# A split-precision decoder trunk: the first weight sum by an adding DMA, one more Strassen pair per unit, Strassen's products in the branch and first output unit

## The chip, the cores and the metric

One core of one Trainium2 chip. The time is the device time of one execution in microseconds. Engines are named as the profile does: PE (TensorE matmuls), PEld (its weight loads), DVE (VectorE), ACT (ScalarE), POOL (GpSimd), SP (SyncE, which issues most DMAs).

## The reference

One layer, 256 rows of width 4096, all in float32:

```python
u = rmsnorm(h, norm_w)
proj = u @ w_in                        # 4096 x 24576
a_q, a_f, a_i, a_g, b_q, b_k, b_v, b_g, gate_a, gate_b = jnp.split(proj, ...)
o_a = rmsnorm(hgrn2_mix(a_q, a_f, a_i, lb)) * silu(a_g)            # 16 heads of 128
o_b = rmsnorm(diff_attention(b_q, b_k, b_v, lam, slopes)) * 0.8 * silu(b_g)   # 8 heads of 256
y = sigmoid(gate_a) * (o_a @ w_branch_a) + sigmoid(gate_b) * (o_b @ w_branch_b)
out = rmsnorm(h + y @ w_out, final_w)
```

Nearly all the work is the four weight products: 256 rows against 512 MB of weights, each used once.

## The kernel before

**Pieces.** All weights are laid out on the host as 512 pieces, "pairs": two blocks of 128 rows of k beside two blocks of 512 columns, that is 128 partitions x 2048 floats (1 MB), the four blocks of 512 in the order B12, B11, B21, B22. Pairs are grouped in units of 1024 output columns. In order: 16 mixer units of 16 pairs (8 groups of two; the first 4 groups feed the recurrence, the next 4 the attention), 8 gate units of 16, 8 half branch units of 8 (4 branch units, each first a then b), 4 output units of 16. `plan` lists them and `run` walks it: per pair it asks for loads up to `LOAD_AHEAD` pairs ahead, splits chunks up to `stream.ahead` ahead, issues the matmuls, then `post(n)` and one or two items of the queue `todo` (`later`, `step`). Items that use PE run only at pairs 14, 15, 0, 1 and 2.

**Split precision.** A float32 weight w is used as hi + lo, each rounded for the fast matmul format: ACT copies hi (L165), DVE forms lo = w - hi (L166). The left operands (u, o, y) are held as hi and lo too, and each block product is three matmuls: hi by hi, hi by lo, lo by hi (`mm`, L289), 512 columns each, into one of 8 PSUM banks.

**Plain and Strassen pairs.** The output of a unit is 2 row blocks x 2 column blocks, banks 0 to 3. A plain pair has two chunks (one per k block) of 1024 columns; each chunk goes to four banks, 24 matmuls in all. A pair of kind "S" is multiplied by Strassen's scheme in Winograd's form: seven block products, 21 matmuls, into banks 0, 1, 2 and P1, p5, P6, P7, with four chunks (1024, 1024, 512 and 1024 columns) in the order of `ORDER`. Its weight sums are made by DVE in `sums`: w0 + w1 (L146), T = w0 - w3 into a tile of its own (L147), and T taken from w1 and w2 at once (L151). Its left sums are formed once per k pair in `s_form` (four DVE operations of 128x128, a copy by ACT, a difference by DVE) and kept in the pools `sp` and `sp2`. The product banks P1 to P7 are evicted after the unit's last S pair into four tiles of the pool `gp` (L313 to L324) and added to banks 0 to 3 at the unit's end. Kinds before: 6 S pairs (`SPLIT`) in mixer units 3 to 15 and gate units 0 and 1; 9 (`SPLIT_G`) in gate units 2 to 6; none in gate unit 7 and the branch units; none in the first output unit and 7 (`Y_SPLIT`) in the three others. 156 of 512.

**Queues and buffers.** Raw pieces have 3 buffers (`wraw`), filled by SP's queue, one DMA per pair except at the start; a buffer is free when the pair's last chunk is split. Split chunks have 5 pairs of tiles in the mixers and 7 afterwards. POOL's queue stores the gates, o, y and h to DRAM, loads y, and masks scores. The order of instructions on each engine is made by a scheduler at build time; splits and evictions get priority (`tc.high_priority`).

**Ends of units.** The last pair of a unit is held and its four blocks are finished one by one, so that banks finish some 1.4 us apart. In the branch units the two halves use different sets of four banks (`bank2`, `bank`), as does the first output unit.

Of the kernel before, what the change touches and what calls it, by code (L numbers as in the profile page):

```python
# [17 lines left out]
P = 128  # L18
D = 4096
S = 256  # L20
# [17 lines left out]
SPLIT_AHEAD = 3  # L38
# [5 lines left out]
def trunk_kernel(ctx, tc, xT, x, nw, w_mix, w_gate, w_branch, w_out, lbt, hnw, lamv, slw, fw, out):  # L44
# [8 lines left out]
    wt = ctx.enter_context(tc.tile_pool(name="wt", bufs=1))  # L53
    sp = ctx.enter_context(tc.tile_pool(name="sp", bufs=6))
# [6 lines left out]

    def bank2(b):
        return bank(("P1", "p5", "P6", "P7")[b])
# [32 lines left out]
    class Stream:  # L96
# [3 lines left out]

        def __init__(self):
# [19 lines left out]
        def load_to(self, n):  # L121
            while self.loaded < min(n, len(self.src)):
# [19 lines left out]
        def sums(self, i, c):  # L142
            w = self.raw[i]
            if c == 0:
                t = self.raw[i, "T"] = wt.tile([P, 512], F32, name="wt", tag="wt")
                dve.tensor_tensor(w[:, 0:512], w[:, 0:512], w[:, 512:1024], op=ALU.add)  # L146
                dve.tensor_tensor(t, w[:, 0:512], w[:, 1536:2048], op=ALU.subtract)  # L147
            if c == 2:
                t = self.raw[i, "T"]
                b = w[:, 512:1536].rearrange("p (a c) -> p a c", a=2)  # L150
                dve.tensor_tensor(b, b, t.unsqueeze(1).to_broadcast([P, 2, 512]), op=ALU.subtract)  # L151

        def split_to(self, n):
            while self.done < min(n, len(self.chunks)):
# [12 lines left out]
                if c == (3 if self.kind[i] == "S" else 1):  # L167
                    del self.raw[i]
                    self.raw.pop((i, "T"), None)
# [96 lines left out]
    ORDER = (("p5", "P1"), (0, 1), ("P6",), ("P7", 2))  # L266
# [4 lines left out]
    def wide_unit(srcs, kinds, pf, sf, bank, final, post=None, tail=1, kt0=0, pre=None):  # L271
# [62 lines left out]
        def fn(n, c, hi, lo):  # L334
            if pre and c == 0:
                pre(n)
            if kinds[n] == "S":
                for i, b in enumerate(ORDER[c]):
# [4 lines left out]
                    else:  # L343
                        s = {"p5": 0, "P6": 1, "P7": 2, 1: 3}[b]
                        uh, ul = (sf[n][:, s, a, :] for a in range(2))
# [8 lines left out]
            for blocks in ([[(t, m)] for t in range(2) for m in range(2)] if tail == 1  # L354
# [86 lines left out]
    SPLIT = (4, 6, 8, 10, 12, 13)  # L441
    SPLIT_G = (0, 2, 4, 6, 8, 10, 12, 13, 14)
    us = {}
    s_pools = [sp] * 6
# [19 lines left out]
    def more_sums(n):  # L464
        if n == 0:
            s_pools[:] = [sp2] * 3
# [4 lines left out]
    oh, ol = [], {}  # L471
# [559 lines left out]
```

## Time and profile before

| | |
|---|---|
| median of 3 runs | 2794.47 us (2794.36 to 2796.64) |
| the profiled execution | 2795.3 us, its span 2793.6 us |
| granted PE clock | 0.999 |
| busy share PE / PEld / DVE / ACT / POOL | 99% / 82% / 79% / 57% / 3% |
| HBM read, written | 571.5 MB, 24.1 MB |
| DMA share of SP's queue, of POOL's queue | 56.3%, 2.8% |

The span runs from the first to the last instruction; the execution's time has 1.7 us around it. In a row of instructions the figures are the count, busy time in us, mean ns of one, idle time of the engine just before them, and what ended that idle time. A window row gives, for a stretch, its length, then busy us and count per engine, the granted clock, the DMA engines' mean busy share, and GB/s. Matmuls overlap in PE's pipeline: a row of 0.39 us is one matmul's way through, and the time from one to the next is shorter.

### The profile page before, as it was taken

To read this page: it belongs to the slowest core of one execution; us is meant where nothing else is said; L and a number is where in the kernel's file an instruction comes from. 1 tells how busy PE (TensorE), PEld (TensorE's weight loads), DVE (VectorE), ACT (ScalarE), POOL (GpSimd) and SP (SyncE) were. 2 spreads that over 40 slices of the span, in tenths; PEclk is the share of its full clock that TensorE was granted. 3 is DMA by queue.
4 is the path that set the end of the run, shared out by engine and by line. 5 is a ranking of instruction groups with operands and counts; after the bars stand their busy time and mean duration, and the time that the engine had idled before them with its cause. 6 is when DMAs were issued, how large, how long until landed. Compare 5 with 4: busy or idle time off the path is not lost.

```text
span 2793.6 us, 32659 instructions
## 1 busy us (share of the span) xinstructions
PE 2770.9 (99%) x12418; PEld 2285.5 (82%) x12418; DVE 2219.3 (79%) x2502; ACT 1578.5 (57%) x1877; POOL 75.0 (3%) x124
## 2 busy tenths in 40 slices
PE   9999999999999999999999999999999999999998
PEld 7888888888888888888888888778888888888886
DVE  6784888888888888888888999999855555668997
ACT  7664656556556555565556555555553444445554
POOL 0010000000000000000000000000000000010000
PEclk9999999999999999999999999999999999999999
DMA  9555555554555555555456555555676666665665
GB/s 351 190 179 192 181 195 189 211 203 181 196 189 208 198 177 203 194 198 201 181 192 239 224 199 208 226 219 203 253 260 220 230 223 234 240 244 212 249 250 217
DMA packets 96767, 597.76 MB, mean 214 GB/s; under 512 B 11857, under 2 KB 12129, under 8 KB 31201
## 3 DMA queue, kind: packets, MB, share of 16 engines
q1 hardware_dynamic: 88272, 566.29, 56.3%
q0 software_dynamic: 8336, 29.38, 2.8%
q8 instruction: 97, 1.59, 0.2%
q14 instruction: 62, 0.50, 0.1%
HBM read 571.51 MB, written 24.12 MB: 213 GB/s over the span
## 4 chain that ended last, share of the span: by engine, by line
PE 84%; DVE 10%; DMA 3%; issue 1%; ACT 1%; POOL 0%; DVEq 0%; ACTq 0%; POOLq 0%
PE ps_w L289 82%; DVE lo L166 7%; DMA w<-in_w_gate 2%; DVE w L151 1%; ACT hi L165 1%; DMA w<-in_w_out 1%; DVE w L146 1%; PE ps_q L742 1%; DVE wt L147 0%; PE ps_sc L825 0%; PE ps_s L906 0%; DVE ut L372 0%; PE ps_o L840 0%; PE ps_y L541 0%; PE ps_t L701 0%
## 5 line engine op out<-in xcount | busy, mean ns | idle before, releaser
L165 ACT ACTIVATE hi<-w 128x1024 fp32r<-128x1024 f32 (+1 forms) x1184 | 1215.1, 1053 | 1073.9 <-PE ps_w L289 598.4
L166 DVE TENSOR_TENSOR lo<-w,hi 128x1024 fp32r<-128x1024 f32 (+1 forms) x1184 | 1415.4, 1219 | 437.1 <-ACT hi L165 423.8
L289 PE MATMUL ps_w<-hi,u 128*128 128x512 f32 x4794 | 1538.4, 391 | 1.7 <-ACT hi L165 1.6
L289 PEld LDWEIGHTS ps_w<-hi,u 128*128 128x128 f32 x4794 | 900.1, 188 | 190.3 <-ACT hi L165 3.0
L289 PE MATMUL ps_w<-lo,u 128*128 128x512 f32 x2397 | 935.0, 390 | 0.9 <-DVE lo L166 0.9
L289 PEld LDWEIGHTS ps_w<-lo,u 128*128 128x128 f32 x2397 | 450.2, 188 | 98.2 <-DVE lo L166 6.5
L289 PE MATMUL ps_w<-hi,sf 128*128 128x512 f32 x1248 | 437.0, 390 | 0.7 <-ACT hi L165 0.7
L289 PE MATMUL ps_w<-hi,oh 128*128 128x512 f32 x1024 | 317.1, 390 | 0.0
L289 PEld LDWEIGHTS ps_w<-hi,sf 128*128 128x128 f32 x1248 | 234.3, 188 | 50.1 <-ACT hi L165 1.4
L289 PE MATMUL ps_w<-hi,y 128*128 128x512 f32 x814 | 258.1, 389 | 0.0
L289 PE MATMUL ps_w<-lo,sf 128*128 128x512 f32 x624 | 244.3, 392 | 4.9 <-DVE lo L166 4.6
L289 PEld LDWEIGHTS ps_w<-hi,oh 128*128 128x128 f32 x1024 | 192.3, 188 | 39.6
L289 PE MATMUL ps_w<-lo,oh 128*128 128x512 f32 x512 | 199.2, 389 | 0.0
L151 DVE TENSOR_TENSOR w<-w,wt 128x1024 f32<-128x1024 f32 x156 | 190.4, 1220 | 0.3
L289 PEld LDWEIGHTS ps_w<-hi,y 128*128 128x128 f32 x814 | 152.8, 188 | 31.6
L289 PE MATMUL ps_w<-lo,y 128*128 128x512 f32 x407 | 158.4, 389 | 0.0
L289 PEld LDWEIGHTS ps_w<-lo,sf 128*128 128x128 f32 x624 | 117.1, 188 | 34.4 <-DVE lo L166 10.5
L146 DVE TENSOR_TENSOR w<-w 128x512 f32<-128x512 f32 x156 | 107.4, 690 | 46.5 <-DMA w<-in_w_mix 33.3
L165 ACT ACTIVATE hi<-wt 128x512 fp32r<-128x512 f32 x156 | 97.9, 627 | 36.9 <-PE ps_w L289 23.0
L289 PEld LDWEIGHTS ps_w<-lo,oh 128*128 128x128 f32 x512 | 96.2, 188 | 19.8
L147 DVE TENSOR_TENSOR wt<-w 128x512 f32<-128x512 f32 x156 | 107.5, 689 | 2.6
L166 DVE TENSOR_TENSOR lo<-wt,hi 128x512 fp32r<-128x512 f32 x156 | 107.1, 686 | 0.0
(206 smaller groups left out, 1040.6 us busy)
## 6 DMA issues: line engine op xcount, KB each, us to landing
w<-in_w_mix SPq DMA_DIRECT2D x252, 1024.0 KB, 4.8
w<-in_w_gate SPq DMA_DIRECT2D x128, 1024.0 KB, 4.9
w<-in_w_branch SPq DMA_DIRECT2D x64, 1024.0 KB, 4.9
w<-in_w_out SPq DMA_DIRECT2D x64, 1024.0 KB, 4.9
gl<-g_dram SPq DMA_DIRECT2D x32, 256.0 KB, 2.7
g_dram<-ut POOLq DMA_DIRECT2D x28, 256.0 KB, 5.3
o_dram<-s POOLq DMA_DIRECT2D x8, 512.0 KB, 6.0
ol<-o_dram SPq DMA_DIRECT2D x16, 256.0 KB, 5.4
```

The costliest lines, as they stand in the source:

```text
L146: dve.tensor_tensor(w[:, 0:512], w[:, 0:512], w[:, 512:1024], op=ALU.add)
L147: dve.tensor_tensor(t, w[:, 0:512], w[:, 1536:2048], op=ALU.subtract)
L151: dve.tensor_tensor(b, b, t.unsqueeze(1).to_broadcast([P, 2, 512]), op=ALU.subtract)
L165: act.activation(hi[:, k : k + m], t[:, k : k + m], AF.Copy)
L166: dve.tensor_tensor(lo[:, k : k + m], t[:, k : k + m], f32(hi[:, k : k + m]), op=ALU.subtract)
L289: pe.matmul(ps[b], a, w, start=first, stop=left[b] == 0)
L742: pe.transpose(ps[:, j], r[:, j * P : (j + 1) * P], ident)
```

## The change

The first weight sum w0 + w1 is no longer made by DVE: an S pair's load is cut into its first 512 columns and the other 1536, and a third DMA, issued by POOL with addition, reads w1 from DRAM a second time and adds it onto w0 in the buffer. The second sum is written over w3 in place, after the chunk that needs the raw w2 and w3; the chunk order changes so that this raw chunk comes first. `SPLIT` gets 7 pairs, `SPLIT_G` 10 (no longer pair 0, but 1); the branch halves get 2 S pairs each, the first output unit 3. Tiles of the mixers go (the sums of squares are made by ACT's accumulation, scaling is one DVE operation per segment, other tiles are used again), the splits run four chunks ahead there, and blocks finish in the order (0,1), (0,0), (1,1), (1,0), which is also that of the first use in the next unit. Both sets of banks are no longer exchanged.

```diff
-SPLIT_AHEAD = 3
+SPLIT_AHEAD = 4
...
     def load_to(self, n):
...
-                if i > 1:
+                if self.kind[i] == "S":
+                    self.load_part(i, 0, 512)
+                    self.load_part(i, 512, PIECE - 512)
+                    pool.dma_start(t[:, 0:512], self.src[i][:, 512:1024], accum_op=ALU.add)
+                elif i > 1:
...
-        def sums(self, i, c):
+        def sums(self, i):
             w = self.raw[i]
-            if c == 0:
-                t = self.raw[i, "T"] = wt.tile([P, 512], F32, name="wt", tag="wt")
-                dve.tensor_tensor(w[:, 0:512], w[:, 0:512], w[:, 512:1024], op=ALU.add)
-                dve.tensor_tensor(t, w[:, 0:512], w[:, 1536:2048], op=ALU.subtract)
-            if c == 2:
-                t = self.raw[i, "T"]
-                b = w[:, 512:1536].rearrange("p (a c) -> p a c", a=2)
-                dve.tensor_tensor(b, b, t.unsqueeze(1).to_broadcast([P, 2, 512]), op=ALU.subtract)
+            t2 = w[:, 1536:2048]
+            dve.tensor_tensor(t2, w[:, 0:512], t2, op=ALU.subtract)
+            b = w[:, 512:1536].rearrange("p (a c) -> p a c", a=2)
+            dve.tensor_tensor(b, b, t2.unsqueeze(1).to_broadcast([P, 2, 512]), op=ALU.subtract)
...
+                    o = c * HALF
                     if self.kind[i] == "S":
-                        self.sums(i, c)
-                    t = self.raw[i, "T"] if c == 2 else self.raw[i][:, (0, 1024, 0, 512)[c] :]
+                        if c == 2:
+                            self.sums(i)
+                        o = (1024, 0, 1536, 512)[c]
+                    t = self.raw[i][:, o:]
...
-    ORDER = (("p5", "P1"), (0, 1), ("P6",), ("P7", 2))
+    ORDER = ((0, 1), ("p5", "P1"), ("P6",), ("P7", 2))
...
-                plain(n, c, hi, lo, [(0, 0), (0, 1), (1, 0), (1, 1)] if c else [(0, 1), (1, 1), (0, 0), (1, 0)])
+                plain(n, c, hi, lo, [(t, m if c else 1 - m) for t in range(2) for m in range(2)])
...
-            for blocks in ([[(t, m)] for t in range(2) for m in range(2)] if tail == 1
+            for blocks in ([[(t, 1 - m)] for t in range(2) for m in range(2)] if tail == 1
...
-    SPLIT = (4, 6, 8, 10, 12, 13)
-    SPLIT_G = (0, 2, 4, 6, 8, 10, 12, 13, 14)
+    SPLIT = (4, 6, 7, 9, 10, 12, 13)
+    SPLIT_G = (1, 3, 4, 6, 7, 9, 10, 12, 13, 14)
...
+    SPLIT_B = (3, 5)
...
-        p_form(oh[n // 2], 2 * (n % 2), ol.pop(n))
+        f = ol.pop(n)
+        p_form(oh[n // 2], 2 * (n % 2), f)
+        if n % 8 in SPLIT_B:
+            os[n] = s_form(f)
...
+        def gated(t, n, ps, c, dst):
+            if c is not None:
+                dve.tensor_tensor(c, ps, c, op=ALU.add)
+                ps = c
+            dve.tensor_tensor(dst, ps, g[t, n], op=ALU.mult)
...
-        wide_unit([w_branch[0, q, n] for n in range(8)], PLAIN[:8], oh, None, bank2, a_final, post)
-        wide_unit([w_branch[1, q, n] for n in range(8)], PLAIN[:8], oh, None, bank, b_final, post_b, kt0=16)
+        wide_unit([w_branch[0, q, n] for n in range(8)], mix(8, SPLIT_B), oh, os, bank, a_final, post)
+        wide_unit([w_branch[1, q, n] for n in range(8)], mix(8, SPLIT_B), oh, os, bank, b_final, post_b, kt0=16)
...
-        kinds = PLAIN if q == 0 else mix(16, Y_SPLIT)
-        wide_unit([w_out[q, n] for n in range(16)], kinds, y, ys, bank if q else bank2, final, post, 3 if q == 3 else 1)
+        kinds = mix(16, Y_SPLIT if q else Y_SPLIT[4:])
+        wide_unit([w_out[q, n] for n in range(16)], kinds, y, ys, bank, final, post, 3 if q == 3 else 1)
...
             def apply():
-                o3 = fl(o).rearrange("p (n c) -> p n c", c=seg)
-                dve.tensor_tensor(o3, o3, T["ss"].unsqueeze(2).to_broadcast([P, n, seg]), op=ALU.mult)
-                dve.tensor_tensor(fl(o), fl(o), fl(T["silu"]), op=ALU.mult)
+                for i in range(n):
+                    c = slice(i * seg, (i + 1) * seg)
+                    dve.scalar_tensor_tensor(fl(o)[:, c], fl(o)[:, c], ss[:, i : i + 1], fl(T["silu"])[:, c],
+                                             op0=ALU.mult, op1=ALU.mult)
...
-                    act.activation(rows(T["o"])[:, tb], pf, AF.Copy)
-                    act.activation(rows(T["sq"])[:, tb], pf, AF.Square)
+                    o = rows(T["o"])[:, tb]
+                    for h in range(HPG):
+                        i = tb * HPG + h
+                        act.activation(o[:, h * P : (h + 1) * P], ps[:, h], AF.Square, accum_out=T["ss"][:, i : i + 1])
+                    act.activation(o, pf, AF.Copy)
```

In the branch units the four row sums of a and b are now queued as one item (`add_rows`) ahead of the four transposes, which use the spare banks.

More of the change, by code (lines that the diff above doesn't have):

```diff
@@ L517, in branch_unit @@
     def branch_unit(q):
-        rows, g = {}, {}
+        rows, g, merge = {}, {}, []
         def g_load(br):
@@ L614, in final @@
                 last_rows[t, n] = tile_
-                if n == 1:
+                if (t, 1 - n) in last_rows:
                     out_rows(t)
-            if t == 0 and n == 1:
+            del xr[t, n]
+            if t == 0 and not xr:
                 io_x(1)
@@ L748, in final @@
                     T["gv"[n]] = big("gv"[n])
-                if t == 1 and n == 1:
+                if t == 1 and n == 0:
                     for f in then:
```

110 lines of the change are left out of this document (57 added, 53 removed).

## The prediction

> **What bounds the kernel now.** Read first: the share of each engine and the chain that ended last.
>
> ```profile
> span 2793.6 us, 32659 instructions
> PE 2770.9 (99%) x12418; PEld 2285.5 (82%) x12418; DVE 2219.3 (79%) x2502; ACT 1578.5 (57%) x1877; POOL 75.0 (3%) x124
> PE 84%; DVE 10%; DMA 3%; issue 1%; ACT 1%; POOL 0%; DVEq 0%; ACTq 0%; POOLq 0%
> PE ps_w L289 82%; DVE lo L166 7%; DMA w<-in_w_gate 2%; DVE w L151 1%; ACT hi L165 1%; DMA w<-in_w_out 1%; DVE w L146 1%; PE ps_q L742 1%; DVE wt L147 0%; PE ps_sc L825 0%; PE ps_s L906 0%; DVE ut L372 0%; PE ps_o L840 0%; PE ps_y L541 0%; PE ps_t L701 0%
> ```
>
> TensorE's weight matmuls are the chain for 82% of the span; VectorE's split of the weights is 7%. Where that 7% lies is asked of the stages, by windows cut where the count of L289's matmuls says a unit begins (366 for a mixer unit, 357 for gate units 2 to 6, 192 for half a branch unit, 363 for an output unit).
>
> ```profile
> core 0: us, PE busy (x) PEld busy (x) DVE busy (x) ACT busy (x) POOL busy (x), PEclk, DMA share, GB/s
> 1587.63:1668.55 80.92, 80.92 (x359) 67.01 (x357) 75.85 (x85) 47.90 (x56) 1.61 (x3) 1.00 0.60 219
> 1668.55:1751.85 83.30, 82.34 (x358) 66.63 (x357) 78.61 (x85) 48.32 (x56) 2.16 (x4) 1.00 0.57 214
> 1751.85:1835.12 83.27, 82.11 (x359) 66.64 (x357) 77.92 (x85) 50.40 (x58) 2.16 (x4) 1.00 0.56 214
> 1835.12:1920.15 85.03, 82.46 (x358) 66.54 (x357) 80.36 (x88) 47.84 (x55) 2.16 (x4) 1.00 0.57 212
> 1920.15:2003.01 82.86, 82.15 (x358) 66.63 (x357) 77.87 (x84) 51.00 (x57) 2.16 (x4) 1.00 0.58 215
> 2003.01:2090.99 87.98, 87.33 (x385) 72.02 (x384) 52.97 (x54) 46.30 (x56) 3.49 (x7) 1.00 0.78 276
> 2134.51:2178.03 43.52, 43.52 (x193) 36.05 (x192) 23.05 (x22) 16.86 (x17) 0.00 (x0) 1.00 0.59 209
> 2444.59:2533.46 88.87, 88.87 (x402) 73.76 (x400) 54.72 (x67) 41.74 (x51) 7.82 (x14) 1.00 0.62 223
> 2615.78:2698.07 82.29, 82.29 (x365) 68.14 (x364) 75.93 (x84) 46.22 (x57) 3.23 (x6) 1.00 0.65 237
> 627.74:715.47 87.73, 87.73 (x410) 73.05 (x408) 75.53 (x82) 57.89 (x70) 2.54 (x2) 1.00 0.54 196
> ```
>
> The branch half (seventh row) is TensorE and nothing else: 43.52 us for 192 matmuls is 0.2267 us each, at a granted clock of 1.00. At that rate 357 matmuls are 80.9 us. Gate unit 2 takes that; units 3 to 6 take 83.3, 83.3, 85.0 and 82.9, and the five together 415.4 where TensorE needs 404.7. So 10.7 us of stall lie there, with VectorE at 76 to 80 of 81 us. Mixer units (last row), branch and output units have TensorE busy throughout with VectorE at 53 to 92%. What TensorE waits for in gate units 3 to 6:
>
> ```profile
> PEld ps_w L289 <- DVE lo L166: 8.8, 11, 1.3
> PE ps_w L289 <- DVE lo L166: 3.9, 7, 0.9
> PEld ps_w L289 <- DVE ut L372: 1.3, 4, 0.4
> ```
>
> The split is late there, the eviction of banks hardly.
>
> **The change, part by part.**
>
> *Fewer matmuls.* A plain pair is 2 chunks x 4 blocks x 3 = 24 matmuls, a Strassen pair 7 x 3 = 21. More Strassen pairs: one in each of the 13 mixer units with Strassen (6 to 7), one in gate units 0 and 1, one in each of gate units 2 to 6 (9 to 10), two in each of the 8 branch halves, three in the first output unit: 13 + 2 + 5 + 16 + 3 = 39. 39 x 3 = 117 matmuls at 0.2267 us: **-26.5 us**. All of it lies on TensorE's path. In the mixer, branch and output units, 34 of the 39 pairs, nothing but TensorE binds now, so 102 x 0.2267 = 23.1 us need only that VectorE stays under it.
>
> *VectorE.* The rows of its work (a run gives the pitch without overlap):
>
> ```profile
> 1794.86 5.76 DVE L166 TENSOR_TENSOR lo<-w,hi 128x1024 fp32r<-128x1024 f32 x5
> 1754.91 2.48 DVE L372 TENSOR_TENSOR ut<-ps_w,ut 128x512 f32<-128x512 f32 x4
> L146 DVE TENSOR_TENSOR w<-w 128x512 f32<-128x512 f32 x156 | 107.4, 690 | 46.5 <-DMA w<-in_w_mix 33.3 <-DMA w<-in_w_gate 9.9 <-DMA w<-in_w_out 2.7
> L151 DVE TENSOR_TENSOR w<-w,wt 128x1024 f32<-128x1024 f32 x156 | 190.4, 1220 | 0.3
> L382 DVE TENSOR_TENSOR s<-yl 128x128 f32<-128x128 f32 x7 | 2.0, 288 | 8.5 <-DMA yl<-y_dram 8.5
> L388 DVE TENSOR_TENSOR sf<-s,sf 128x512 fp32r<-128x512 f32 x16 | 11.0, 687 | 2.1 <-ACT sf L387 2.1
> L373 ACT ACTIVATE ut<-ut 128x512 f32<-128x512 f32 x28 | 16.7, 626 | 6.3 <-DVE ut L372 6.3
> ```
>
> 128x1024: (5.76 - 1.22) / 4 = 1.135 us. 128x512: (2.48 - 0.69) / 3 = 0.60. A plain pair is 2 x 1.135 = 2.27; a Strassen pair now 3 x 0.60 (L146, L147, short lo) + 4 x 1.135 = 6.34, and 5.74 when L146 goes to the DMA. Mixer unit: 6 x 6.34 + 10 x 2.27 = 60.7 becomes 7 x 5.74 + 9 x 2.27 = 60.6, no change. Gate units 2 to 6: 9 x 6.34 + 7 x 2.27 = 73.0 becomes 10 x 5.74 + 6 x 2.27 = 71.0, so busy time falls from 78.7 (mean of units 3 to 6) to 76.7, while TensorE falls from 80.9 to 354 x 0.2267 = 80.3. The slack grows from 2.2 to 3.6 us a unit. I take half of the 10.7 us of stall as recovered: **-5**; the bounds are 0 and -10.7. Half, because the wait of lo on ACT's hi stays, and three Strassen pairs in a row stay before the unit's end (12, 13, 14). Output units 1 to 3 lose 7 x 0.60 on VectorE: worth nothing, TensorE binds. Branch half: + 2 x (5.74 - 2.27) + 8 x 0.60 for the four Strassen evictions and four more adds = 11.7, so 34.8 of its new 186 x 0.2267 = 42.2 us. First output unit: 54.7 + 3 x 3.47 + 4.8 = 70 of about 87. Forming four left operands for the branch (per pair 4 x 0.29 by the row of L382, and 0.69, together 1.85) falls in gate unit 7, at 53 of 88 us. All covered; if that cover went, they would cost their own size.
>
> *Banks.* The first output unit and the first half of each branch unit leave the second set of four banks. A unit now meets the banks of the last one, but evictions and first use come in one order (1, 0, 3, 2), so each bank has 3 blocks of 6 matmuls (4.1 us) less the 0.68 us steps of the next unit, at the least 2.0 us, before it is needed; an eviction is 0.69. 0, bounded by the 1.3 us of L372 per four units either way.
>
> *Mixer details.* The sum of squares moves to ACT (at most 58 of 88 us), the fused scaling saves VectorE about 1 us a group: 0 on the path. The products of heads and their transposes keep their count. Splitting four chunks ahead and not three adds lead at the start of mixers only: 0.
>
> *The adding DMA.* Each Strassen load becomes 256 KB and 768 KB on SP's queue and, behind the first's landing, 256 KB added on POOL's queue. The second chunk cannot be split before that lands. No row shows an accumulating DMA; nearest are these, of the same size.
>
> ```profile
> gl<-g_dram SPq DMA_DIRECT2D x32, 256.0 KB, 2.7
> w<-in_w_mix SPq DMA_DIRECT2D x252, 1024.0 KB, 4.8
> L500 POOL DMA_DIRECT2D yl<-y_dram x16: 536/538/773, 2364.5 to 2468.2; - x16
> DMA to landing us min/median/max: 3.4/5.1/6.8
> ```
>
> 2.7 + 5.1 = 7.8 us from SP's issue to the sum's landing, between 2.7 + 3.4 = 6.1 and, if the addition doubles the price, 2.7 + 10.2 = 12.9. I take 5.1, the median of the only POOL loads into SBUF of that size. When it is wanted, by a Strassen pair of a mixer (pair 8 of the ninth unit) and of a gate unit:
>
> ```profile
> 743.16 0.33 SPq L133 DMA_DIRECT2D w<-in_w_mix  x1
> 751.01 1.06 ACT L165 ACTIVATE hi<-w 128x1024 fp32r<-128x1024 f32 x1 [0.31 <-PE ps_w L289]
> 752.36 2.01 ACT L165 ACTIVATE hi<-w 128x1024 fp32r<-128x1024 f32 x2 [0.29 <-PE ps_w L289]
> 759.59 0.39 PE L289 MATMUL ps_w<-hi,sf 128*128 128x512 f32 x1
> 1695.31 0.33 SPq L133 DMA_DIRECT2D w<-in_w_gate  x1
> 1703.19 2.94 ACT L165 ACTIVATE hi<-w 128x1024 fp32r<-128x1024 f32 x3
> ```
>
> In the mixer the second chunk's hi starts about 753.4, 10.2 us after the issue, and TensorE begins the pair 6.2 us after that: 2.4 us of margin, and then a lead of 5.3 us (6.2, and 1.4 for the first chunk's 6 matmuls, less 1.06 + 1.22 for hi and lo). In the gate unit it starts at about 1705.1, the third of the run, 9.8 us after. So 7.8 us is hidden in both. Queued behind it on POOL are the gates' stores, masks of the mixers, y loads and, at a gate unit's end, the reverse: the add for the next unit's pair 1 may stand behind four stores that wait for ACT's last sigmoid. Then it would issue about 2.2 us after the unit's end (0.69 for the add of L372, 0.63 for the sigmoid of L373, the rest queueing), land 5.1 later, and its chunk be split 2.3 later, 9.6, where TensorE wants it after 30 matmuls, 6.8: 2.8 us, in five units 14. Bounds 0 and +14; I take **+2**, nearer to zero, as these stores become ready with the unit's last blocks and POOL is 3% busy. [...]
>
> Sum: -26.5 - 5 + 2 = -29.5. The profiled execution took 2795.3 us, 1.7 more than its span; 2765.8 by it. The median of the runs is 0.8 lower, 2794.47: **2765.0 us**.
>
> **The rivals.**
>
> *Slower: the add is late.* A buffer's loop for a Strassen pair is 2.7 + X + 1.06 (hi) + 0.60 + 1.135 + 1.135 + 0.60 + 1.135 = 8.4 + X, for a plain pair 4.8 + 1.06 + 2 x 1.135 = 8.1. With three buffers a gate unit needs at least (10 x (8.4 + X) + 6 x 8.1) / 3: 61 us at X = 5.1, TensorE's 80.3 at X = 10.8. Beyond it each further microsecond costs 3.3 us a unit, 17 in five; the -29.5 is spent at X = 12.6. At X = 15 it is 2765 + 70 = 2835. For it: an addition reads its destination too, and no row bounds it. Against: the slowest of the 16 POOL loads is 6.8. Chance 0.11.
>
> *Slower still: three small transfers move at a worse rate.* [...] By rows: 2.7 and 4.8 us for 256 and 1024 KB are 0.79 MB in 2.1 us, 374 GB/s, and 214 GB/s at a share of 0.57 is 375. A gate unit would move 17.8 MB + 10 x 0.26, the adds twice, 23 MB or 61 of 80 us. If a Strassen pair's pieces went at half that rate it would be 104 us, 2765 + 118 = 2883. Against: gate unit 7 moves 276 GB/s with 256 KB loads among them, TensorE busy 87.3 of 88.0. Chance 0.02.
>
> *Gates worse.* VectorE's order is made anew, adjacent Strassen pairs eat the lead (2 x 5.74 against 9.5), and the add behind the stores costs the full 14: -26.5 + 0 + 14 and a few us more, 2772 to 2788. For it: stall already stands there. Chance 0.20.
>
> *Gates free.* All 10.7 recovered, and no add late: 2794.5 - 37.2 = 2757; 2752 to 2758 with the rest of the stalls. Chance 0.14.
>
> *No gain.* The pairs are there but the time is not, since the branch and output units turn bound by VectorE: it would need 7 us more per branch half than the 34.8 counted. Chance 0.03.
>
> **How the numbers follow.** The likeliest case, 2758 to 2772, has 0.50. Range 2752 to 2788: it takes in the two gate cases, 0.84 together, and leaves out the late add. 0.2%, 5.6 us, is about what can be told here: faster 0.86, same 0.03, slower 0.11 (the two transfer rivals, less the part where the lateness only eats the gain).
>
> **What would show it.** TensorE's count falls by 117 to 12301; branch halves take 42.2 to 44 us with 186 weight matmuls; gate units 2 to 6 take 80.3 to 81.5; the adding DMA's issues read x195 and land near 5; VectorE's first sum (L146) is gone and its later waits on a weight DMA stay under 1 us each in mixers. Wrong would be: a landing of the add above 10, TensorE waiting for hi or lo of the second chunk in mixers, gate units over 83, or branch halves that no longer run at 0.2267 us a matmul.

## The result, and the profile after

The changed kernel takes 2973.47 us, median of 4 runs (2970.2 to 2978.81), beside 2794.92 for the kernel before on the same chip: a ratio of 1.0637, interval 1.0624 to 1.0649. It was forecast at 2765.0 with a range to 2788, so the forecast missed by 208 us and on the wrong side. The profiled execution has a span of 2972.3 us. Its shares and its chain that ended last:

```profile
PE 2829.9 (95%) x12301; PEld 2274.0 (77%) x12301; DVE 2303.1 (77%) x2624; ACT 1649.4 (55%) x2058; POOL 245.8 (8%) x319
PE 37%; DMA 18%; DVE 12%; ACT 4%; issue 4%; POOL 0%; ACTq 0%; POOLq 0%; DVEq 0%; SPq 0%
PE ps_w L288 36%; DVE lo L166 8%; DMA w<-in_w_gate 8%; DMA w<-in_w_mix 6%; ACT hi L165 4%; DMA w<-in_w_out 3%; DVE w L148 2%; DVE w L146 1%; DMA xr<-in_x 0%; DMA yl<-y_dram 0%; PE ps_s L922 0%; PE ps_q L756 0%; PE ps_y L558 0%; DVE ut L628 0%; DVE ut L371 0%
core 0: 2972.3 us, clock 0.984
```

TensorE has exactly the 117 matmuls fewer that were counted (12301), yet its share of the chain fell from 84% to 37%, and weight DMAs now hold 17%, where it was 3%. The last row is the mean granted clock: 0.984, where before it was 0.999. The stages, cut where the count of L288's matmuls says a unit begins (the mixers with Strassen, gate units 2 to 6, one branch half, all of the branch):

```profile
286.10:1480.29 1194.19, 1161.43 (x5154) 935.03 (x5153) 954.76 (x1083) 705.22 (x914) 90.75 (x110) 0.99 0.65 206
1665.21:2159.36 494.15, 441.07 (x1771) 340.78 (x1772) 389.32 (x402) 256.44 (x291) 51.80 (x68) 0.95 0.66 205
2246.81:2288.97 42.16, 42.16 (x188) 34.91 (x186) 33.01 (x35) 22.19 (x26) 2.56 (x4) 1.00 0.72 246
2246.81:2589.85 343.04, 343.04 (x1537) 283.81 (x1536) 277.36 (x312) 177.40 (x199) 25.46 (x34) 1.00 0.73 245
```

The same cut of every kernel run here, in us (the last column to the last weight matmul of the unit):

| kernel | mixers 0-2 | mixers 3-15 | gates 0-1 | gates 2-6 | gate 7 | branch | out 0 | out 1-3 |
|---|---|---|---|---|---|---|---|---|
| before | 272.0 | 1141.6 | 167.4 | 415.4 | 88.0 | 353.6 | 88.9 | 247.7 |
| forecast | 272.0 | 1132.8 | 166.0 | 409.0 | 88.0 | 342.7 | 86.9 | 247.7 |
| after | 279.3 | 1194.2 | 184.9 | 494.1 | 87.5 | 343.0 | 92.0 | 278.2 |
| e2 adding DMA, old pairs | 273.5 | 1151.8 | 178.5 | 450.9 | 87.2 | 353.6 | 88.9 | 270.3 |
| e10 six split tiles | 278.2 | 1181.0 | 177.1 | 484.2 | 88.5 | 343.0 | 89.8 | 275.3 |
| e4 four load buffers | 280.1 | 1160.4 | 166.8 | 417.3 | 87.2 | 346.4 | 91.9 | 249.7 |
| e3 load in two, VectorE sum | 278.2 | 1183.4 | 175.6 | 452.5 | 88.7 | 343.1 | 88.3 | 251.9 |
| e1 one load, VectorE sum | 280.6 | 1152.0 | 168.1 | 438.2 | 88.6 | 343.1 | 89.1 | 254.5 |
| e5 POOL loads, nothing added | 278.4 | 1143.2 | 166.8 | 413.2 | 87.0 | 343.5 | 87.1 | 247.2 |
| e7 the same, six split tiles | 279.3 | 1132.2 | 165.7 | 407.4 | 87.6 | 342.9 | 87.1 | 246.6 |
| e6 branch only | 272.0 | 1144.3 | 167.5 | 426.9 | 87.6 | 343.1 | 88.5 | 252.7 |
| e6b more in the branch | 272.4 | 1143.0 | 167.5 | 425.3 | 87.6 | 341.2 | 96.4 | 251.6 |
| e8 early sum, late T | 272.0 | 1138.0 | 167.1 | 436.2 | 87.7 | 344.4 | 87.2 | 260.7 |
| e9 the same, seven pairs | 278.3 | 1134.8 | 165.7 | 436.4 | 88.3 | 343.5 | 89.6 | 255.6 |
| e11 before's stream, six split tiles | 272.5 | 1138.6 | 167.1 | 421.4 | 88.0 | 343.0 | 88.4 | 249.0 |

Of the parts that got more Strassen pairs only the branch did as forecast. Output units 1 to 3 kept their matmuls and lost 30.5 us: there only the way of the weight sums and the orders of chunks and blocks had changed. What the transfers and the adds took (size, and median from issue to landing in us; the rows of POOLq are the adds, which L127 issues):

```profile
w<-in_w_mix SPq DMA_DIRECT2D x93, 256.0 KB, 3.5
w<-in_w_mix POOLq DMA_DIRECT2D x91, 256.0 KB, 5.5
w<-in_w_gate POOLq DMA_DIRECT2D x64, 256.0 KB, 5.9
```

And who waited (total wait in us, times, longest wait in us). Before:

```profile
ACT hi L165 <- DMA w<-in_w_gate: 26.3, 17, 5.0
ACT hi L165 <- DMA w<-in_w_mix: 22.9, 20, 2.6
```

After:

```profile
ACT hi L165 <- DMA w<-in_w_gate: 138.7, 52, 6.7
ACT hi L165 <- DMA w<-in_w_mix: 67.3, 42, 3.1
ACT hi L165 <- DMA w<-in_w_out: 65.4, 31, 6.7
PEld ps_w L288 <- DVE lo L166: 136.7, 159, 2.1
PE ps_w L288 <- DVE lo L166: 78.0, 121, 1.8
PE ps_w L288 <- ACT hi L165: 29.5, 12, 6.0
```

TensorE's waits for hi and lo are what the forecast named as a sign of being wrong; a landing of the add above 10 us, its other sign, did not come (the slowest of the 195 took 9.1). One pair shows how they come about: pair 10 of the ninth mixer unit, right behind pair 9, both Strassen.

```profile
786.47 0.80 SPq L134 DMA_DIRECT2D w<-in_w_mix  x2
788.74 0.33 SPq L134 DMA_DIRECT2D w<-in_w_mix  x1
790.48 0.84 POOL L127 DMA_DIRECT2D w<-in_w_mix  x1 [7.22 <-DMA w<-in_w_mix]
796.94 1.06 ACT L165 ACTIVATE hi<-w 128x1024 fp32r<-128x1024 f32 x1 [1.97 <-DMA w<-in_w_mix]
798.03 1.23 DVE L166 TENSOR_TENSOR lo<-w,hi 128x1024 fp32r<-128x1024 f32 x1 [1.62 <-ACT hi L165]
801.77 0.50 PE L288 MATMUL ps_w<-lo,sf 128*128 128x512 f32 x1 [0.62 <-DVE lo L166]
803.57 2.60 SPq L134 DMA_DIRECT2D w<-in_w_mix  x3
803.60 0.72 PE L288 MATMUL ps_w<-lo,sf 128*128 128x512 f32 x1 [0.77 <-DVE lo L166]
```

SP issues the pair's two parts at 786.47. POOL issues the add 4.0 us later, when the next pair's 1 MB is already under way (788.74); ACT, which had stood for 1.97 us, starts the second chunk another 6.5 us later, 10.5 after the first issue. VectorE stood behind ACT. Then the rest of the pair's splitting still has to be done, and the buffer is free at 803.57, when SP at once issues the load three pairs on. That buffer was held for 17.1 us. TensorE's work for three pairs there (two Strassen, one plain: 66 matmuls of 0.2267 us) is 15.0. So the ring of three buffers turns slower than TensorE, its lead runs out, and it stands at the third and fourth chunk.

A freed buffer is loaded again 0.03 us later (median), so the time that a buffer is held is the pace of three pairs, whoever sets it. That the add sets it here is seen at the second chunk: over the 13 units, ACT starts it at pairs 10 and 13 in the median 0.10 us after the sum landed. Of the 279 us that ACT stood on weight DMAs in the whole run, 175.5 stand before the second chunk of a Strassen pair, that is, on the add.

### The profile page after: what moved, and what is told of

The parts are those of the page before. It is cut to its first block, busy times and chain, and to the rows that moved or that the text cites. A ratio compares the mean times of both kernels' runs of the same rounds, so it can differ in the third digit from the quotient of the medians.

```text
span 2972.3 us, 33913 instructions
## 1 busy us (share of the span) xinstructions
PE 2829.9 (95%) x12301; PEld 2274.0 (77%) x12301; DVE 2303.1 (77%) x2624; ACT 1649.4 (55%) x2058; POOL 245.8 (8%) x319
## 4 chain that ended last, share of the span: by engine, by line
PE 37%; DMA 18%; DVE 12%; ACT 4%; issue 4%; POOL 0%; ACTq 0%; POOLq 0%; DVEq 0%; SPq 0%
PE ps_w L288 36%; DVE lo L166 8%; DMA w<-in_w_gate 8%; DMA w<-in_w_mix 6%; ACT hi L165 4%; DMA w<-in_w_out 3%; DVE w L148 2%; DVE w L146 1%; DMA xr<-in_x 0%; DMA yl<-y_dram 0%; PE ps_s L922 0%; PE ps_q L756 0%; PE ps_y L558 0%; DVE ut L628 0%; DVE ut L371 0%
## 5 line engine op out<-in xcount | busy, mean ns | idle before, releaser
L165 ACT ACTIVATE hi<-w 128x1024 fp32r<-128x1024 f32 (+1 forms) x1418 | 1362.7, 993 | 1174.0 <-PE ps_w L288 436.1
L166 DVE TENSOR_TENSOR lo<-w,hi 128x1024 fp32r<-128x1024 f32 (+1 forms) x1418 | 1584.0, 1146 | 551.9 <-ACT hi L165 546.2
L288 PE MATMUL ps_w<-hi,u 128*128 128x512 f32 x4594 | 1498.5, 395 | 7.5 <-ACT hi L165 6.3
L288 PEld LDWEIGHTS ps_w<-hi,u 128*128 128x128 f32 x4594 | 873.5, 190 | 193.8 <-issue 5.3
L288 PE MATMUL ps_w<-lo,u 128*128 128x512 f32 x2297 | 904.1, 394 | 0.2 <-DVE lo L166 0.2
L288 PE MATMUL ps_w<-hi,sf 128*128 128x512 f32 x1560 | 562.7, 400 | 23.4 <-ACT hi L165 23.2
L288 PEld LDWEIGHTS ps_w<-lo,u 128*128 128x128 f32 x2297 | 437.1, 190 | 94.0 <-DVE lo L166 1.3
L288 PE MATMUL ps_w<-lo,sf 128*128 128x512 f32 x780 | 323.2, 414 | 79.3 <-DVE lo L166 77.5
L288 PEld LDWEIGHTS ps_w<-hi,sf 128*128 128x128 f32 x1560 | 295.9, 190 | 104.8 <-ACT hi L165 52.4
L288 PE MATMUL ps_w<-hi,oh 128*128 128x512 f32 x864 | 274.1, 390 | 0.0
L288 PEld LDWEIGHTS ps_w<-lo,sf 128*128 128x128 f32 x780 | 147.6, 189 | 158.6 <-DVE lo L166 133.5
L288 PE MATMUL ps_w<-hi,y 128*128 128x512 f32 x784 | 252.9, 392 | 13.2 <-DVE ut L625 12.4
L148 DVE TENSOR_TENSOR w<-w 128x1024 f32<-128x1024 f32 x195 | 238.6, 1224 | 4.8
L288 PEld LDWEIGHTS ps_w<-hi,oh 128*128 128x128 f32 x864 | 162.2, 188 | 34.1 <-DVE ut L533 0.7
L288 PEld LDWEIGHTS ps_w<-hi,y 128*128 128x128 f32 x784 | 147.9, 189 | 45.9 <-issue 13.6
L288 PE MATMUL ps_w<-lo,oh 128*128 128x512 f32 x432 | 168.1, 389 | 0.0
L288 PE MATMUL ps_w<-lo,y 128*128 128x512 f32 x392 | 153.9, 393 | 0.5 <-DVE lo L166 0.3
L127 POOL DMA_DIRECT2D w<-in_w_mix x91 | 76.7, 842 | 864.8 <-DMA w<-in_w_mix 577.4
L127 POOL DMA_DIRECT2D w<-in_w_gate x64 | 54.1, 845 | 554.9 <-DMA w<-in_w_gate 186.2
L288 PEld LDWEIGHTS ps_w<-lo,oh 128*128 128x128 f32 x432 | 81.1, 188 | 16.4
L288 PEld LDWEIGHTS ps_w<-lo,y 128*128 128x128 f32 x392 | 74.0, 189 | 17.1 <-DVE lo L166 1.9
```

The costliest lines, as they stand in the source:

```text
L127: pool.dma_start(t[:, 0:512], self.src[i][:, 512:1024], accum_op=ALU.add)
L148: dve.tensor_tensor(b, b, t2.unsqueeze(1).to_broadcast([P, 2, 512]), op=ALU.subtract)
L165: act.activation(hi[:, k : k + m], t[:, k : k + m], AF.Copy)
L166: dve.tensor_tensor(lo[:, k : k + m], t[:, k : k + m], f32(hi[:, k : k + m]), op=ALU.subtract)
L288: pe.matmul(ps[b], a, w, start=first, stop=left[b] == 0)
```

## The experiments

The question is which part of the change costs the time: the extra pairs or the adding DMA; and in the latter the wait for the chain of two transfers, the cut load, or the traffic. The experiments e2, e3, e4, e5, e7 and e10 are one run each.

**The sum given back to VectorE (e1).** All 195 Strassen pairs stay; one 1 MB load, and the first sum on VectorE ahead of the second chunk.

```diff
-    pool.dma_start(t[:, 0:512], self.src[i][:, 512:1024], accum_op=ALU.add)
...
+    if c == 1:
+        dve.tensor_tensor(w1[:, 0:512], w1[:, 0:512], w1[:, 512:1024], op=ALU.add)
```

> The changed kernel with the first weight sum back on VectorE (ahead of the second chunk) and one 1 MB load per pair; all 195 Strassen pairs, orders and tiles as changed. Theory A (the chain first part, wake of POOL, addition lands after VectorE wants the sum; VectorE then waits in order and TensorE runs dry): the waits go, a mixer unit with Strassen takes 85 to 87 us on the mean of two against 90.5, branch halves stay at 42.2, and gate units 2 to 6 are bound by VectorE (76.7 + 10 x 0.60 = 82.7 busy) at 83 to 87 us each: 2775 to 2800 in all. Rival B (adjacent Strassen pairs and the new orders are at fault, not the DMA): mixer units stay near 90 and gate units near 100, 2930 or more.

Measured: 2832.8 (2830.39 to 2834.47), 1.0126 times before, interval 1.0109 to 1.0143. Of the 178.6 us lost, 140.7 are gone with the adding DMA, cut load included, so rival B is out. But theory A's range is missed by 33 us: mixers take 88.6 us a unit and gate units 2 to 6 87.6, and the extra pairs there still bring nothing.

**The adding DMA alone (e2).** The pairs of before in every unit, none in the branch (`SPLIT`, `SPLIT_G` as before, `SPLIT_B = ()`).

> The changed kernel with the adding DMA but the Strassen pairs of before (6 in mixers, 9 in gate units 2 to 6, none in branch units and the first output unit: 156). Theory A: a sum is late where two Strassen pairs are adjacent or the buffers come free in a burst. Mixer units lose only at pairs 12 and 13 (1 to 2 us a unit), output units 1 to 3, whose pairs are the same, stay at 91 to 94 us against 82.3, gate units still lose at 12 to 14 and at the unit's start: 2850 to 2900. Rival B (adjacent pairs and orders alone): 2790 to 2810 with output units at 82. Rival C (the smaller pieces and the bytes of the additions load the DMA engines): loss in proportion to the pairs, 156 of 195 of 205 us, 2955.

Measured: 2876.86, in theory A's range. With before's pairs the adding DMA, its cut load and the new orders cost 80 us together (the kernel before took 2797.01 in this round); e6 below, which has the orders without the DMA, puts some 14 of them on the orders. With the new pairs 117 matmuls fewer cost another 97. Mixers take 1151.8 with the old pairs and 1194.2 with the new; that it is the neighbours (6, 7 and 9, 10), and not the mere count, is argued from the landings pair by pair further down.

**The load cut in two, nothing added (e3).** e1 with 256 and 768 KB on SP's queue.

> As the run with the sum back on VectorE (2832.8 us), but an S pair's load is still cut into 256 and 768 KB on SP's queue, without the addition. Rival C (small pieces load the queue and the DMA engines badly): most of the changed kernel's loss stays, 2880 or more. Theory A (the loss is the serial chain to the sum): within 12 us of 2833.

Measured: 2882.61, 50 us above e1 (on another chip, where the kernel before took 2796.70 beside 2797.01). Theory A's 12 us are missed, and rival C's 2880 came out, though the DMA engines were no busier in e3, 0.52 and 0.54 of the time in both. The mixers and gate units 2 to 6 of e1, then of e3:

```profile
286.61:1438.65 1152.04, 1144.78 (x5154) 931.97 (x5153) 998.67 (x1173) 702.97 (x914) 14.88 (x19) 1.00 0.52 193
1606.77:2044.92 438.15, 418.86 (x1771) 330.13 (x1769) 413.53 (x452) 254.16 (x290) 10.77 (x20) 0.99 0.54 202
```

```profile
284.39:1467.75 1183.36, 1158.56 (x5155) 927.14 (x5153) 1002.01 (x1173) 703.43 (x914) 12.86 (x19) 1.00 0.52 188
1643.35:2095.80 452.45, 424.42 (x1771) 327.75 (x1769) 414.28 (x452) 253.39 (x289) 10.81 (x20) 0.99 0.54 195
```

The traffic is the same. A buffer of mixer pairs 10 to 12 is held (first issue to last lo, medians over the 13 units) 15.9 us in e1 and 17.2 to 17.7 in e3, where TensorE needs 15.0. The landings explain some of it. In e1 and in e3:

```profile
w<-in_w_mix SPq DMA_DIRECT2D x252, 1024.0 KB, 4.8
```

```profile
w<-in_w_mix SPq DMA_DIRECT2D x91, 768.0 KB, 5.0
```

The 768 KB land later though they are less, and are issued some 0.4 us behind the 256 KB (two issues take 0.80 us above): 0.6 to 0.8 us. VectorE's waits from 286 to 2160 us show where that goes (L156 in e1 and L159 in e3 are the first sum):

```profile
DVE w L156 <- DMA w<-in_w_mix: 11.0, 13, 2.8
```

```profile
DVE w L159 <- DMA w<-in_w_mix: 53.6, 62, 2.8
```

The sum of a pair stands in VectorE's order ahead of the last lo of the Strassen pair before it (seen in the twelfth mixer unit). While it waits for its load, that lo waits too, and with it the buffer that the lo would free. So e3's loss goes, at least in part, through an instruction that the changed kernel does not have.

**Lead or buffers (e4, e10).** e4 has a fourth load buffer and pays for it after the mixers with one pair of split tiles and one chunk of lead; e10 has one more pair of split tiles in the mixers and gate unit 0, and three buffers.

```diff
-    wraw = ctx.enter_context(tc.tile_pool(name="wraw", bufs=3))      # e4
+    wraw = ctx.enter_context(tc.tile_pool(name="wraw", bufs=4))
...
-    stream.ring = [(whi, wlo)] * 5 + [(whi2, wlo2)] * 2
+    stream.ring = [(whi, wlo)] * 5 + [(whi2, wlo2)]
...
-    stream.ahead = 5
+    stream.ahead = 4
...
-SPLIT_AHEAD = 4                                                      # e10
+SPLIT_AHEAD = 5
...
-    whi = ctx.enter_context(tc.tile_pool(name="whi", bufs=5))        # wlo the same
+    whi = ctx.enter_context(tc.tile_pool(name="whi", bufs=6))
...
-    stream.ring = [(whi, wlo)] * 5 + [(whi2, wlo2)] * 2
+    stream.ring = [(whi, wlo)] * 6 + [(whi2, wlo2)]
```

> The changed kernel with four raw buffers for three; to make room, one pair of late split tiles for two and four chunks ahead for five after the mixers (the mixers are untouched by that). Theory A: each load is issued a pair earlier, some 5 us, more than the sum is late by, so mixer units go to 85 to 87 us (mean of two) from 90.5, and the gate units, though with less lead, below 95. Rivals B and C: mixer units stay near 90.

> The changed kernel with its adding DMA, and six pairs of split tiles (five chunks split ahead) in mixers and gates in place of five; nothing else. Theory A, the lead: the sum is late by a chunk's worth, and one more chunk of lead hides it: mixers 3 to 15 fall from 1194 to below 1160, gate units 2 to 6 from 494 to below 450, the run to 2840 to 2900. Theory B, the buffers' loop: a Strassen pair's load buffer is held for its load, the add and the splits, three buffers turn too slowly whatever is split ahead, and only a fourth buffer helps (as it did: 2820.65): gate units 2 to 6 stay above 480 and the run within 25 of 2973.

Measured: 2820.65 and 2937.28. Mixers and gate units 2 to 6 of e4:

```profile
286.94:1447.37 1160.43, 1144.95 (x5154) 932.66 (x5153) 951.56 (x1083) 701.04 (x914) 91.31 (x110) 1.00 0.68 212
1614.15:2031.45 417.30, 406.56 (x1771) 330.66 (x1770) 389.32 (x407) 257.15 (x294) 52.39 (x69) 1.00 0.81 246
```

and of e10:

```profile
284.41:1465.46 1181.05, 1150.85 (x5154) 933.52 (x5153) 949.62 (x1083) 704.32 (x915) 88.08 (x110) 1.00 0.66 209
1642.59:2126.78 484.19, 440.38 (x1771) 341.98 (x1772) 387.75 (x401) 254.82 (x289) 51.88 (x68) 0.95 0.67 208
```

The buffer brings 153 us with the same adds and the same traffic, and ACT's waits on the add fall from 175.5 us to 38.9. Theory A's gate units came out (83.5 us each), its mixers did not: 89.3 us a unit over all 13, from 91.9, where 85 to 87 was expected of two. e10 took 36 us off, which is in neither range, though theory B's gate units, above 480, came out. Its expectation counts the gates among the stages with more lead, which is not so: after gate unit 0 both kernels have seven pairs of tiles and split five chunks ahead. Only 22 of the 36 us lie in the mixers and gate units 0 and 1; the other 14, of which 9.9 are in gate units 2 to 6, come from units whose tiles and lead are the same, so a stage can differ by that much between two such runs without a cause that is known. The loop of the load buffers is the main limit, the lead the smaller one. The DMA share of 0.81 in e4's gates says too that the transfers could go faster all along.

**No chain between the two transfers (e5, e7).** POOL loads the second block plainly in place of the first, waiting for the buffer alone; w0 is left out of the sum. The same bytes go through POOL's queue, 256 KB a pair less through SP's. e7 adds the sixth split tile.

```diff
-    self.load_part(i, 0, 512)
-    pool.dma_start(t[:, 0:512], self.src[i][:, 512:1024], accum_op=ALU.add)
+    pool.dma_start(t[:, 0:512], self.src[i][:, 512:1024])
```

> The changed kernel with POOL's DMA as a plain load of w1 into the place of w0 + w1, the first 256 KB not loaded by SP, so that POOL waits for the buffer alone; w0 is left out of the sum and the output is not the reference's. The same count of POOL DMAs, and 256 KB less per Strassen pair. Theory A: the chain is 5 to 6 us for 8 to 12, and mixer units go to 85 to 87, gate units 2 to 6 to 80 to 85: 2765 to 2800. If POOL's queue or its descriptors are the cost (rival D: it stands behind other waits, or writing descriptors slows VectorE), it stays above 2900.

> As the run with the plain POOL load (2786.9 us; w0 left out of the sum, the output is not the reference's), with six pairs of split tiles in the mixers for five and splits five chunks ahead for four (afterwards seven and five as before). Theory A'': the small stalls of 0.5 us at the second of two adjacent Strassen pairs, which eat the 0.68 us of the seventh pair there, are a lack of lead; units 3 to 15 fall from 1143 to 1130 to 1137 us. If instead VectorE's rate alone sets them, they stay within 2 us of 1143.

Measured: 2786.87 and 2769.25, each as its theory A had it. Mixers and gates of e7:

```profile
285.49:1417.72 1132.23, 1130.74 (x5154) 936.50 (x5153) 948.50 (x1083) 700.13 (x915) 61.28 (x110) 1.00 0.56 197
1583.41:1990.78 407.37, 404.17 (x1771) 331.42 (x1770) 383.51 (x399) 251.70 (x288) 36.21 (x67) 1.00 0.62 217
```

e7 is the forecast's kernel with the sum free and in time, and one pair of split tiles more: mixers 1132.2 (1132.8 was forecast), gates 2 to 6 407.4 (409.0), branch 342.9 (342.7). e5, without that tile, is 22 us above the forecast, and its mixers gain nothing from their seventh pairs (1143.2, before 1141.6). So neither the matmuls nor POOL's queue as such were the large error; the 186.6 us between e5 and the changed kernel are the chain of two transfers, and whatever the one transfer of 256 KB brings that e5 has less per pair. Held buffers of mixer pairs 10 to 13 take 15.4 us in e5 and e7, 17.2 in the changed kernel.

**Only the branch (e6, e6b).** Before's pairs in mixers and gates, VectorE's sum as in e1, the branch's new products; e6b has three pairs per branch half and five in the first output unit.

```diff
-    SPLIT = (4, 6, 7, 9, 10, 12, 13)
+    SPLIT = (4, 6, 8, 10, 12, 13)
...
-    SPLIT_B = (3, 5)            # e6b only
+    SPLIT_B = (2, 4, 6)
```

> The first sum on VectorE, the pairs of before in mixers (6) and gate units 2 to 6 (9), Strassen in the branch halves (2 each) and the first output unit (3), orders and tiles as changed. Theory A': where TensorE is the bound and VectorE has slack the saved matmuls are saved time, elsewhere a pair more is eaten by the lead. Branch -10.3 to -10.9, first output unit -1 to -2, the rest as before: 2780 to 2786, ratio 0.995 to 0.997. If the changed order of chunks and blocks costs by itself (rival B), mixers and gate units lose 10 us or more and it is no faster than before.

> As the run before with three pairs in each branch half (2, 4, 6) and five in the first output unit (4 to 12): 10 pairs more, 30 matmuls, 6.8 us less by theory A', 2773 to 2780. If the four eviction tiles, held while y is loaded and formed in the last branch half and the first output unit, bring waits, that part gives back 3 us or more.

Measured: 2799.85, 1.0009 times before (1.0000 to 1.0018), and 2804.94, 1.0030 (1.0018 to 1.0041). Theory A' missed in both, and e6 came out as its rival B had it: the branch gave its 10.5 us, but gate units 2 to 6 rose to 426.9 and output units 1 to 3 to 252.7, with before's pairs in them. So the changed orders and the later places of the sum and of T cost by themselves. In e6b the branch gained 2 us more and the first output unit lost 7.5 against before, more than the 3 that its expectation feared.

**Where the difference T is formed (e8, e9, e11).** e8: the sum ahead of the first chunk again, before's order of products, six split tiles; T still in place at the third chunk. e9: e8 with a seventh pair per mixer. e11: before's sums altogether, with a tile for T.

```diff
-    t2 = w[:, 1536:2048]                 # e8, e9: at the third chunk
-    dve.tensor_tensor(t2, w[:, 0:512], t2, op=ALU.subtract)
+    t = self.raw[i, "T"] = wt.tile([P, 512], F32, name="wt", tag="wt")    # e11: at the first
+    dve.tensor_tensor(t, w[:, 0:512], w[:, 1536:2048], op=ALU.subtract)
```

> Strassen's products in the branch (pairs 3 and 5) and three in the first output unit, mixers and gates with the pairs of before (6 and 9), one 1 MB load, the first weight sum on VectorE ahead of the pair's first chunk as before, the first chunk's products in the order of before, and six pairs of split tiles. Against the run with the sum ahead of the second chunk and five tiles (2799.85): theory A, that run lost its 10.6 us of the branch because the first sum and two subtractions stood between the first and the third chunk, late in the pair: here gate units 2 to 6 take 410 to 417 in place of 427, output units 1 to 3 247 to 249 in place of 252.7, the run 2776 to 2784. Theory B, the Strassen products of the branch and the banks' new order cost what they bring: 2792 to 2800, with gate units above 422 or output units above 251.

> The same, and seven Strassen pairs in each mixer (pair 2 added, none of them adjacent but 12 and 13). Theory A, TensorE binds in mixers: 13 x 0.68 = 8.8 us fewer in mixers 3 to 15, less up to 7 us that the seventh left sum costs in the first three mixers beside POOL's masks: 0 to 9 us under the run with six. Theory B, VectorE has no room for a seventh pair with its own first sum (7 x 6.34 + 9 x 2.27 = 64.8 us of 83 and the mixer's other work): 5 to 25 us above it.

> The splitting of weights as before in every point but six pairs of split tiles: one 1 MB load, the first sum and the difference T (into a tile of its own) on VectorE ahead of the pair's first chunk, the pairs of before in mixers and gates; with it Strassen's products in the branch and in three pairs of the first output unit. The run with T formed in place ahead of the third chunk (2814.07) lost 20.8 us in gate units 2 to 6 and 13 in output units 1 to 3 against before. Theory A, T was late there (TensorE's waits stand at the third chunk) and each such wait of some 2 us was followed by some 10 us at half the granted clock: here gate units 2 to 6 take 408 to 418, output units 1 to 3 247 to 249, and the run 2774 to 2784. Theory B, the new order of banks or the branch's pairs disturb the gates and output units, T has no part in it: gates above 425, the run above 2792.

Measured: 2814.07 (1.0065, 1.0051 to 1.0079), 2808.5 (1.0046, 1.0034 to 1.0059) and 2788.25 (0.9978, 0.9969 to 0.9987). Gate units 2 to 6 of e8, then of e11:

```profile
1583.73:2019.98 436.25, 418.95 (x1786) 335.12 (x1785) 395.57 (x425) 246.36 (x280) 10.73 (x20) 0.99 0.55 205
```

```profile
1584.25:2005.68 421.43, 411.55 (x1786) 332.79 (x1785) 391.69 (x425) 243.37 (x280) 10.46 (x20) 1.00 0.57 212
```

The same pairs, the same work on each engine; T two chunks later, and in w3's place and not in a tile of its own, costs 14.8 us here and 11.7 in output units 1 to 3. What expectation A of e8 took for enough, an early first sum, was not the point: e8 is 14.2 us slower than e6, whose sum is later, and misses both of its ranges. The early T was the point. (The 10 us at half clock in e11's expectation are too long: the clock of 0.96 and 0.68 in e8's windows 2550 to 2556 and 2556 to 2566 makes 7 us of half clock.) e11 misses its own range by 4 us, as its gates stay 6.0 above before's; tiles and lead are before's there and the order of blocks in the banks is new, but a difference of this size in one profile each may have no cause in the change, and it stays open. Still, e11 beats both kernels: 7.5 us under before. e9 is 5.6 us under e8, within its theory A, but by luck: its seventh pair brings 3.2 us in mixers 3 to 15, not 8.8, and costs 6.4 in the first three, while output units 1 to 3, in which nothing changed, were 5.1 faster.

## Why the prediction was wrong, step by step

**Fewer matmuls: right in the branch, too much in the mixers.** The branch gained 10.6 of the 10.9 us counted, at 42.16 us a half (42.2 was said), and its VectorE stayed below that. The rival "no gain" is dead. In the mixers the count came true only with the sum in time and a sixth pair of split tiles (e7); with the sum in time alone (e5) their seventh pairs brought nothing. That nothing but TensorE binds in the mixers, by which the pairs there were counted in full, did not hold for seven pairs: a second step that failed, worth some 10 us.

**The adding DMA, hidden at 7.8 us: the step that failed,** in three of its numbers.
- The first part was put at 2.7 us, from the gate loads; it lands at 3.5. POOL's wake, some 0.6 us more, was not counted.
- The add was put at 5.1. The median is 5.5 (the shortest of the 195 took 3.9), but a median is the wrong number: taken pair by pair in mixers, the add of the first of two neighbours (pairs 6, 9 and 12), which has another pair's load beside it for 0.05 us or less (medians), lands in 4.0 us, that of the second (7, 10 and 13), which runs beside the next load, in 6.3 to 6.4; pair 4, without a neighbour but beside a load too, takes 5.8. The sum is there 8.0 to 8.3 us after the first issue for the one and 10.4 to 10.6 for the other. The second chunk was wanted at 9.8 to 10.2.
- The loop 8.4 + X was compared with TensorE as a mean over a unit's ten Strassen and six plain pairs, giving a limit of X = 10.8. Three buffers average over three pairs, not sixteen. For two Strassen pairs and a plain one TensorE takes 15.0 us, so the limit is 15.0 - 8.4 = 6.6. The measured X at pair 10 is 10.4 - 2.7 = 7.7, the loop by the formula 16.1, by the trace 17.1. The rival "the add is late" had the mechanism; its chance of 0.11 rested on that limit, and its price, 2835 us, was worked out for X = 15. In gate units 2 to 6 the 50 sums are there 11.0 us after the first issue in the mean, X = 8.3, below the limit of 10.8, and yet these units took 98.8 us each.

**The cut load: not costed.** The sum has no term for it. e3 puts 50 us on it beside e1, but through VectorE's first sum, which the changed kernel does not make; there the first chunk of mixer pairs 9, 10, 12 and 13 starts 2.1 to 3.2 us after its 768 KB landed (medians), so the cut does not hold it up, and what the cut alone costs there stays open. The rival of three small transfers had priced it as bandwidth, at half the rate of the rows, which no run shows: 2883 us at 0.02. Bandwidth it was not: e4 moves 246 GB/s with the same pieces.

**The add behind stores, +2: the wrong wait.** At the start of the fifth gate unit:

```profile
1850.80 0.85 POOL L127 DMA_DIRECT2D w<-in_w_gate  x1 [19.66 <-DVE lo L166]
1859.92 1.06 ACT L165 ACTIVATE hi<-w 128x1024 fp32r<-128x1024 f32 x1 [6.71 <-DMA w<-in_w_gate]
1861.03 0.79 PE L288 MATMUL ps_w<-hi,sf 128*128 128x512 f32 x1 [5.43 <-ACT hi L165]
1861.80 0.58 POOL L373 DMA_DIRECT2D g_dram<-ut  x1 [10.14 <-ACT ut L372]
1862.38 0.86 POOL L127 DMA_DIRECT2D w<-in_w_gate  x1
```

The add for pair 1 stands behind no store: it is issued 0.6 us after its first part landed, and takes 9.0 us. ACT stands before that chunk, and the sigmoid that POOL's store waits for comes behind it in ACT's order. TensorE stands for 5.4 us. In gate units 2 to 6 this add took 6.0 to 9.0 us, and each time ACT started the chunk 0.10 us after it landed. Why it is so slow there is not shown; in the unit above two loads of 1 MB, the second in two parts, are under way beside it. The next add, for pair 3, is issued behind that store, as the term had it, in the five units 0.6 to 5.9 us after its first part landed; but its chunk is split only 2.8 to 7.8 us after it has landed, so this path cost nothing. TensorE's waits for hi at the starts of these five units are 24.8 of the 29.5 us shown above, in five of the 12 times, against the 14 us that were the upper bound.

**The clock: not in the sum.** After such a stand (the columns are the stretch, its length, the busy times, then the granted clock):

```profile
1853.00:1861.00 8.00, 2.60 (x12) 1.83 (x10) 1.35 (x2) 1.29 (x3) 0.00 (x0) 0.84 0.71 193
1861.00:1863.00 2.00, 0.90 (x2) 0.40 (x2) 1.99 (x3) 0.63 (x2) 1.20 (x2) 0.50 0.03 14
1863.00:1865.00 2.00, 2.00 (x5) 1.61 (x6) 1.97 (x4) 1.95 (x4) 1.39 (x4) 0.50 0.71 178
1867.00:1869.00 2.00, 2.00 (x7) 1.57 (x6) 0.73 (x1) 1.82 (x2) 0.00 (x0) 0.58 0.46 184
1869.00:1871.00 2.00, 2.00 (x11) 1.64 (x10) 2.00 (x3) 2.00 (x3) 0.00 (x0) 1.00 0.00 0
```

TensorE is busy again from 1863, at half the clock until 1868.7. By the mean clock, (1 - 0.984) x 2972 = 48 us is the most that can have been lost so; but of 93 us at half clock TensorE was busy in 69, so the loss is about 34 us (before, it was busy in none). The whole is 205 us, 178.7 of span and the 26.5 that were saved: TensorE's idle time grew from 22.7 to 142.4 us, which is 120 of them, and its busy time, for fewer matmuls, makes the other 85, in which the clock's 34 are. At this stand the clock went to half at 1858.4, 2.8 us into its 5.4 us, and stayed there for 10.2 us, of which 5.7 follow 1863. What sets these lengths is not shown.

**VectorE's slack in the gates: within its bounds, no more.** With the sum in time gates 2 to 6 fell by 8.0 in e7 and by 2.2 in e5, where 3.4 + 5 was said. Tiles and lead in these units are the same in both, so the half of the 10.7 us that was taken can't be told from these runs.

**Mixers 0 to 2: a term missed.** Forming the seventh left operand costs 6 to 9 us in the first mixers in every kernel with seven pairs, 0 to 1.5 in those with six. e9 beside e8, which differ in that pair alone, shows 6.4. POOL's mask was caught beside it (first row before, the others after):

```profile
180.46 7.05 POOL L828 TENSOR_SCALAR_AFFINE_SELECT sc<-sc 128x512 f32<-128x512 f32 x2 [168.31 <-ACT sc L826]
L842 POOL TENSOR_SCALAR_AFFINE_SELECT s<-s x8: 629/1454/10696, 182.3 to 738.3; 128x512 f32<-128x512 f32 x8
193.08 2.08 PE L855 MATMUL ps_o<-v,s 128*128 128x128 f32 x8 [4.56 <-POOL s L842]
```

The same instruction takes 0.6 to 10.7 us, the longest in the first group, where VectorE forms the left operands densely (busy in 10.2 of the 11.28 us of the first two masks, and in 6.5 of their 7.05 before). The two masks of that group take 7.05 us together before and 11.28 after, which is 4 of the 7 us. What draws them out is not shown: no run here changes VectorE's work beside them alone.

## What to carry over

Hold a ring of n load buffers against n pairs in a row, not against a unit's mean: add up first issue, every transfer chained behind it, the engines' wake (POOL's took some 0.6 us) and the splits, and compare with the compute of the n densest neighbours. Moving an instruction of 0.69 us from VectorE to a chained DMA let the sum be there 10.4 us after the first issue, where 4.8 + 0.69 was possible, to free an engine that was not the limit in most stages. Where the loop binds, another buffer paid more than another tile of lead (153 against 36 us at the most). And the place of a small step counts: one difference of 0.69 us, formed two chunks later and in place, cost 26 us (e8 beside e11).

## What the hardware showed that was not expected

The accumulating DMA of 256 KB into SBUF is not dear in itself: in mixers 4.0 us with hardly another pair's load beside it (pairs 6, 9 and 12) and 6.3 to 6.4 beside the next pair's load (7, 10 and 13). Plain POOL loads of that size took 3.4 to 6.8 before, and those of the same pieces in e5 4.6 in the median of the mixers, so the addition did not double it. What it costs is its wait for the transfer that it adds to. And the clock halved after a stand that was not one long gap. In the mixer of above, the timeline names no wait of TensorE beyond 0.77 us between 801 and 805, eight matmuls in 4 us:

```profile
801.00:803.00 2.00, 1.22 (x4) 0.48 (x3) 1.40 (x3) 1.77 (x2) 0.00 (x0) 1.00 0.80 127
803.00:805.00 2.00, 1.40 (x4) 1.12 (x5) 2.00 (x3) 2.00 (x3) 0.00 (x0) 0.68 0.12 31
805.00:807.00 2.00, 2.00 (x6) 1.63 (x5) 2.00 (x3) 1.07 (x2) 0.00 (x0) 0.50 0.81 297
807.00:809.00 2.00, 2.00 (x10) 1.56 (x10) 1.97 (x3) 0.20 (x1) 0.85 (x1) 0.97 0.95 332
```

The clock was halved all the same for 3.4 us, from 803.7 to 807.1, with TensorE busy throughout: 1.7 us of its work by estimate, which turns a stall of 2 us into one of nearly 4.
